# A two-layer streaming encoder on one core: first norm and first weight splits without GpSimd, and a scheduler with a transfer model and other TensorE prices

## The chip, the core and the metric

The program runs on one core of one Trainium2 chip. The metric is the device time of one execution in microseconds (us); for several runs it is the median. The engines are TensorE (PE; PEld is its weight load), VectorE (DVE), ScalarE (ACT), GpSimd (POOL) and SyncE (SP), which issues the DMAs. Each engine works through its own instructions in order and waits on semaphores for the others.

## The reference

A trunk of two layers over 512 frames, with 16 meta tokens ahead of them (528 rows of 1024 in all). Layer 0 projects the normed input once for two head groups, A (sparse attention with a top-k indexer) and B (gated linear attention in chunks of 64, "GLA"); layer 1 does so for C (retention) and D (stick-breaking attention). Cut to what matters here:

```python
def rms_norm(x, g):
    y = x * rsqrt(mean(x * x, -1) + 1e-6)
    return y * g
...
hn = rms_norm(h, norm_g[layer])
aq, ak, av, ag, iq, ik, iw, bq, bk, bv, bg, ba = split_cols(hn @ w_in, SPLIT_AB)
# indexer: score = sum_h relu(iq_h ik) * iw_h; top 128 keys of each frame, masked softmax over them
# B: chunked gated linear attention over bq, bk, bv with decays from ba
out = concat([oa * silu(ag), ob * silu(bg)]) @ w_out
h = h + out
```

Layer 1 has the same frame, and a last norm ends the program.

## The kernel before, in words

**Tiles and precision.** Everything stays on chip as 128x528 tiles. A projection of 128 output columns is 48 matmuls: eight blocks of 128 input features, three products each (upper part of the weights by upper part of x, upper by lower, lower by upper; the tiles are `wh`, `wl` for the weights, `hh`, `hl` for x, all in the rounded 32-bit format), each in two halves of 272 and 256 columns. An order row or a profile row `acc<-hh,wh` is such a product.

**Weights.** `load` (L541) brings half a projection's weights (128x512) into a `raw` tile. `split_next` (L562) makes `wh` from it, on GpSimd for the first `PW` tiles and on ACT after that, and `wl` = raw - wh, on GpSimd for the first `PL` tiles and on DVE after that. `PW, PL` stand in L482 as 2, 1. One projection, the "combined tile" (`COMB`, columns of indexer keys, indexer weights and GLA's gate), is put together from three transfers of 64, 8 and 16 columns into a tile that GpSimd has cleared.

**The start.** `consts` (L658) runs 46 warm-up transposes of the identity on PE (`WARM`, L483). `load_x` (L709) loads x in blocks of 128 rows, two 512-wide halves each (`pt`; the meta tokens in `gv`). For a block, `square` (L733) sums the squares of the first half on ACT and of the second half on DVE. `norm` (L744) takes Ln and Exp on ACT and scales the first half on DVE (L749) and the second on GpSimd (L750). `turn` (L752) transposes the blocks of one feature group on PE into a PSUM tile; ACT makes `hh` from it with the norm's gain, DVE makes `hl`. The products of the first indexer tile and of the combined tile are recorded between these steps.

**Order.** The code doesn't issue instructions directly. A recorder (`Recorder`) notes all of them with their dependences, and `issue` (L384) writes them out at the end in the order that a list scheduler finds; so all rows of recorded instructions carry the line of `issue`'s call, L393. `price` (L216) gives each an estimated cost and a matmul its class: contraction rows, plain or rounded operands, and slot length. `deadlines` (L260) walks the program once forward over PE (a matmul's due time is the sum of the slots ahead of it) and once backward (the latest start of every other instruction); these are the priorities. `order` (L285) then places instruction after instruction by the earliest start that its model of each engine gives, with priority among those that can start. `slot` (L376) adds `SWITCH` when PE goes from plain to rounded operands and `ROWS` when the contraction rows differ. Tiles rotate in pools (PSUM tags `x`, `y`, `acc`), and a buffer is given out in program order.

**Later stages.** After the first projections the indexer's scores are computed (about 36 to 80 us), then `topk` (L886) runs scans on DVE (`MAX`, `MATCH_REPLACE`) while PE goes on with values and GLA. `gla_steps` (L1318) is one GLA head: chunk products, a transpose of the key stack, then its meta step, which is a 16x16 product into a PSUM tile `m`, a masked copy of it by DVE (`attm`), a transpose of a 64x16 stack into the same tile, DVE's copy of that, and two small products. DVE then updates the head's state `ss` step by step. `out_ab` (L1410) ends layer 0, `stick` (L1590) is group D, `out_cd` (L1636) ends layer 1.

Of the kernel before, what the change touches and what calls it, by code (L numbers as in the profile page):

```python
# [13 lines left out]
ALU = mybir.AluOpType  # L14
# [152 lines left out]
class Recorder:  # L167
# [48 lines left out]
    def price(self, o):  # L216
        o.mm, o.port = None, False
        n = max([x.free() for x in o.ins + o.outs] or [1])
        sbuf = not any(x.tile.psum for x in o.ins)
        scalar = 65 if any(isinstance(x, View) and x.free() == 1 for x in o.ins) and n > 1 else 0  # L220
        if o.eng == "tensor":
            lhs, rhs = (o.args[1], o.args[2]) if len(o.args) > 2 else (o.kw["lhsT"], o.kw["rhs"])
            turn = o.name == "transpose"
            plain = rhs.dtype == F32
            k, m, n = lhs.shape[0], lhs.free(), rhs.free()
            two = plain and not turn
            o.mm = (k, plain, max(n * 0.455 * (2 if two else 1) + 4, 107 * m / P + 4) + (107 if two and n <= P else 0))
            o.cost = max(273, 170 + 0.4375 * n) if not two else 180 + 1.62 * n
        elif o.eng == "scalar":
            o.cost = (205 if sbuf else 165) + 0.83 * n + (80 if isinstance(o.kw.get("bias"), View) or isinstance(o.kw.get("scale"), View) else 0)  # L230
            if "accum_out" in o.kw:
                o.cost += 200
        elif o.eng == "vector":
            o.port = sbuf and o.name not in ("max", "match_replace")
            if o.name == "tensor_tensor_scan":
                o.cost = 144 + 2.1 * n
            elif o.name in ("tensor_scalar", "tensor_copy") and sbuf:
                o.cost = 160 + 0.52 * n + scalar
            elif o.name == "memset":
                o.cost = 100 + 0.3 * n  # L240
            else:
                o.cost = 148 + 1.05 * n + scalar
            if o.name == "tensor_tensor_reduce" or "accum_out" in o.kw:
                o.cost += 80
            if o.name == "match_replace":
                o.cost += 70
        elif o.eng == "gpsimd":
            o.cost = {"memset": 92 + 0.84 * n, "tensor_tensor": 178 + 2.17 * n}.get(o.name, 194 + 1.5 * n)
        else:
            x = o.outs[0] if o.outs else o.ins[0]  # L250
            kb = n * x.shape[0] / 256
            o.cost = 2000 + kb * (9 if any(y.tile.whole for y in o.outs + o.ins) else 3.5)


    LAT = {"tensor": 55, "vector": 33, "scalar": 34, "gpsimd": 60, "sync": 27}
    OVER = {"vector": -84, "scalar": -103, "gpsimd": -60}
    SWITCH, ROWS = 86, 50
    MARGIN = 300

    def deadlines(self):  # L260


        ops, t, last = self.ops, 0.0, None
        due = {}
        for o in ops:
            if o.eng == "tensor":
                if last is not None:
                    t += self.slot(last, o)
                last = o
            due[o] = t  # L270
        late = {}
        turn = {}
        for o in reversed(ops):
            end = min([late[q] - self.LAT[q.eng] for q in o.succs] + [late[q] - self.LAT[q.eng] for x in o.tiles
                      for q in [turn.get((x.kind, x.at + x.kind.bufs))] if q and q.at > o.at], default=due[o] + 20000)
            start = end - o.cost
            if o.eng == "tensor":
                start = min(start, due[o])
            late[o] = start
            for x in o.tiles:  # L280
                turn[x.kind, x.at] = o
        for o in ops:
            o.pri = due[o] if o.eng == "tensor" else late[o]

    def order(self):  # L285
        ops = self.ops
# [6 lines left out]
        free = dict.fromkeys(self.LAT, 0.0)  # L293
        lists = {e: [] for e in self.LAT}
        last = None
        begun = {}
        result = []

# [15 lines left out]
        while left:  # L314
            best = None
            for e, xs in lists.items():
                pick = None
                base = free[e] + (last.mm[2] if e == "tensor" and last is not None else 0)
                for o in xs:
# [11 lines left out]
                        continue  # L331
                    now = free[e] + (self.slot(last, o) if e == "tensor" and last is not None else 0)
                    start = max(est, now)
                    key = (max(est + (self.MARGIN if e == "tensor" else 0) - base, 0.0), o.pri)
                    if pick is None or key < pick[0]:
                        pick = (key, start, o)
                if pick and (best is None or pick[1] < best[1]):
# [5 lines left out]
            cost = o.cost  # L343
            if e == "vector" and o.port and begun.get("pool", (0, 0))[0] < start < begun.get("pool", (0, 0))[1] - 100:
                cost += begun["pool"][1] - start - 70
            end = start + cost
            ends[o] = end
            o.begin, o.end = start, end
            if e == "tensor":
                free[e], last = start, o  # L350
            elif e == "sync":
                free[e] = start + 430
            else:
                free[e] = end + self.OVER[e]
                if e == "gpsimd":
# [20 lines left out]
    def slot(self, a, b):  # L376
        t = a.mm[2]
        if a.mm[1] and not b.mm[1]:
            t += self.SWITCH
        if a.mm[0] != b.mm[0]:  # L380
            t += self.ROWS
        return t
# [14 lines left out]
class Kernel:  # L397
# [81 lines left out]
    LASTK = 4  # L479


    XL, XC, XN, XW, PW, PL = 2, 9, (0, 1, 1, 2), (1, 4, 7, 10, 13), 2, 1  # L482
    WARM = 46  # L483

    LAG = {"a": 5, "d": 6, "t": 1, "v": 4, "n": 9, "s": 6, "k": 11}
# [223 lines left out]
    def load_x(self):  # L709
# [34 lines left out]
        def norm(b):  # L744
# [2 lines left out]
            r = ms[b][:n]  # L747
            self.rstd(r, r, DM)
            nc.vector.tensor_scalar(x0[:n], x0[:n], r, None, op0=ALU.mult)  # L749
            nc.gpsimd.tensor_scalar(x1[:n], x1[:n], r, 1.0, op0=ALU.mult, op1=ALU.mult)  # L750

        def turn(group, t0, k):  # L752
            tr = self.s()
# [1039 lines left out]
```

## Time and profile before

| what | value |
|---|---|
| time of the kernel before, median of 3 | 663.05 us (662.98 to 663.65) |
| the profiled execution's own time | 663.46 us |
| its span, first to last instruction | 661.7 us |
| mean granted TensorE clock | 0.984 |
| instructions | 12217 |

Busy time over the span:

| engine | us | share | instructions |
|---|---|---|---|
| PE | 636.6 | 96% | 4469 |
| DVE | 484.3 | 73% | 1176 |
| ACT | 405.1 | 61% | 910 |
| POOL | 76.4 | 12% | 124 |

In a row of the timeline stand the start and the busy time, the engine, the line, the operation, what it writes and reads with shapes, and in brackets how long the engine stood idle before it and which engine's tile released it. In a row of the windows stand the stretch, then for PE, PEld, DVE, ACT and POOL the busy time with the count of instructions, then the granted clock as a share of the full one, the mean busy share of the DMA engines and the GB/s they moved. Durations of PE are modelled from pipelined matmuls, so a "busy" PE may be stalled behind a slow clock; spans on POOL are rough.

### The profile page before, as it was taken

What the parts mean: (1) busy time and instruction counts of PE and PEld (TensorE: products, weight loads), DVE (VectorE), ACT (ScalarE), POOL (GpSimd) and SP (SyncE); (2) the same over time, 40 slices, a digit from 0 to 9 for tenths busy, and PEclk for the clock granted to TensorE, in tenths of its full rate; (3) what the DMA queues carried; (4) which work ended last, traced back from release to release, by engine and by line L of the source; (5) the groups of instructions that cost most, each with busy time, mean ns of one, the idle gap of its engine ahead of it and who ended that gap; (6) DMA issues with size and microseconds to landing.
All of it is one profiled execution on the core that took longest, in us unless ns stands there. A gap on an engine that the chain in (4) does not pass through costs nothing.

```text
span 661.7 us, 12217 instructions
## 1 busy us (share of the span) xinstructions
PE 636.6 (96%) x4469; PEld 581.4 (88%) x4469; DVE 484.3 (73%) x1176; ACT 405.1 (61%) x910; POOL 76.4 (12%) x124
## 2 busy tenths in 40 slices
PE   5999999899999999999999999999999999999996
PEld 5879989798899999999899999878988888988884
DVE  4777799899987869679632764699935699955643
ACT  3656563353444877699643675799744699944434
POOL 7101110111000000001121110001200001110030
PEclk8899999799999999999999999999999999999998
DMA  7437222132322323112143272203322203224403
GB/s 217 118 83 224 72 74 72 46 96 65 81 57 75 98 65 97 52 47 65 50 145 112 67 238 81 64 21 93 97 65 64 78 2 104 83 71 149 153 17 127
DMA packets 91104, 59.25 MB, mean 90 GB/s; under 512 B 7315, under 2 KB 81629, under 8 KB 91045
## 3 DMA queue, kind: packets, MB, share of 16 engines
q1 hardware_dynamic: 91044, 58.48, 30.8%
q8 instruction: 35, 0.57, 0.3%
q14 instruction: 25, 0.20, 0.1%
HBM read 53.18 MB, written 6.90 MB: 91 GB/s over the span
## 4 chain that ended last, share of the span: by engine, by line
PE 67%; DVE 18%; ACT 9%; issue 2%; DMA 2%; SPq 0%; DVEq 0%; ACTq 0%
PE acc L393 45%; PE x L393 15%; PE y L393 6%; ACT wt L393 6%; DVE wt L393 5%; DVE st L393 3%; DVE lt L393 3%; DVE wl L393 3%; DVE m L393 2%; DMA pt<-in_x_dram 2%; ACT pt L393 1%; DVE pt L393 1%; ACT ptm L393 1%; ACT st L393 0%; DVE vt L393 0%
## 5 line engine op out<-in xcount | busy, mean ns | idle before, releaser
L393 PE MATMUL acc<-hh,wh 128*128 128x272 f32 (+2 forms) x968 | 246.5, 315 | 3.0 <-ACT hh L393 1.5
L393 PE MATMUL acc<-hh,wl 128*128 128x272 f32 (+2 forms) x968 | 234.2, 302 | 1.9 <-DVE wl L393 1.9
L393 PE MATMUL acc<-hl,wh 128*128 128x272 f32 (+2 forms) x968 | 234.8, 304 | 0.7 <-DVE hl L393 0.5
L393 ACT ACTIVATE wh<-raw 128x512 fp32r<-128x512 f32 x152 | 94.7, 629 | 125.2 <-PE acc L393 110.6
L393 PEld LDWEIGHTS acc<-hh,wh 128*128 128x128 f32 x968 | 159.5, 190 | 10.2 <-issue 3.0
L393 PEld LDWEIGHTS acc<-hh,wl 128*128 128x128 f32 x968 | 158.2, 190 | 8.5 <-DVE wl L393 2.8
L393 PEld LDWEIGHTS acc<-hl,wh 128*128 128x128 f32 x968 | 158.2, 190 | 5.0 <-DVE hl L393 1.5
L393 DVE TENSOR_TENSOR wl<-raw,wh 128x512 fp32r<-128x512 f32 x153 | 109.1, 718 | 57.2 <-ACT wh L393 52.2
L393 ACT ACTIVATE wt<-x 128x272 f32<-128x272 f32 (+3 forms) x100 | 43.0, 453 | 28.4 <-PE x L393 17.8
L393 POOL TENSOR_TENSOR gt<-gt,wt 128x528 f32<-128x528 f32 (+1 forms) x16 | 21.2, 1326 | 322.5 <-ACT wt L393 303.4
L393 PE MATMUL x<-st,st 128*128 128x272 f32 (+6 forms) x240 | 51.5, 292 | 0.1
L393 PE MATMUL x<-ident,wt 128*128 128x128 f32 (+2 forms) x300 | 46.0, 275 | 2.1 <-DVE wt L393 1.2
L393 ACT ACTIVATE wt<-wt 128x528 f32<-128x528 f32 (+3 forms) x74 | 42.9, 603 | 4.7 <-DVE wt L393 4.0
L393 PEld LDWEIGHTS x<-st,st 128*128 128x128 f32 (+2 forms) x240 | 37.5, 185 | 8.8 <-ACT wt L393 3.1
L393 ACT ACTIVATE wt<-wt,tiny 128x272 f32<-128x272 f32 (+5 forms) x64 | 34.7, 561 | 10.3 <-DVE tiny L393 10.0
L393 PEld LDWEIGHTS x<-ident,wt 128*128 128x128 f32 (+2 forms) x300 | 33.7, 139 | 7.0 <-DVE pt L393 1.4
L393 PE MATMUL y<-pt,vt 128*128 128x256 f32 (+1 forms) x288 | 38.6, 277 | 0.0
L393 PEld LDWEIGHTS y<-pt,vt 128*128 128x128 f32 x288 | 36.4, 189 | 1.3 <-DVE pt L393 0.7
L393 ACT ACTIVATE st<-acc 64x528 fp32r<-64x528 f32 (+1 forms) x58 | 34.7, 599 | 1.1 <-DVE lt L393 0.5
L393 DVE TENSOR_TENSOR_SCAN wt<-wt,wt 128x64 f32<-128x64 f32 (+5 forms) x50 | 30.8, 654 | 1.5 <-ACT wt L393 1.3
L393 DVE TENSOR_TENSOR pt<-x,pt 128x384 fp32r<-128x384 f32 (+1 forms) x48 | 28.1, 594 | 2.7 <-ACT pt L393 2.1
L393 ACT ACTIVATE wt<-wt,one 128x528 f32<-128x528 f32 (+3 forms) x42 | 29.5, 705 | 0.2
(191 smaller groups left out, 893.9 us busy)
## 6 DMA issues: line engine op xcount, KB each, us to landing
raw<-in_w_in_ab_dram SPq DMA_DIRECT2D x64, 256.0 KB, 2.8
raw<-in_w_in_cd_dram SPq DMA_DIRECT2D x56, 256.0 KB, 2.9
raw<-in_w_out_ab_dram SPq DMA_DIRECT2D x16, 256.0 KB, 2.8
raw<-in_w_out_cd_dram SPq DMA_DIRECT2D x16, 256.0 KB, 2.6
rep<-rows SPq DMA_DIRECT2D x8, 328.0 KB, 6.8
lt<-rep SPq DMA_DIRECT2D x8, 264.0 KB, 3.0
pt<-in_x_dram SPq DMA_DIRECT2D x8, 256.0 KB, 5.2
wt<-in_x_dram SPq DMA_DIRECT2D x8, 256.0 KB, 3.3
```

The costliest lines, as they stand in the source:

```text
L393: getattr(getattr(self.core, o.eng), o.name)(*[bind(x) for x in o.args], **{k: bind(x) for k, x in o.kw.items()})
```

## The change

It has two parts. In the kernel's code the second half of each block of x is scaled on DVE instead of GpSimd, and `PW, PL` are 0, 0: the first two upper weight tiles are made by ACT and the first lower one by DVE.

In the scheduler, nothing of what is computed differs, but the numbers and rules that set the order do. A matmul's class is 32, 64 or 128 contraction rows, and not the exact number; a slot is 0.45 ns per column. `SWITCH` is 80 and counts only after a matmul (10 after a transpose), `ROWS` is 95. A matmul whose row class is that of the one before gets 2000 ns (`STAY`) off its due time. A transfer's cost is its size times 3.6; the transfers share a modelled wire, so that each ends after the one before it and at least 1900 ns after its issue; one from scratch to scratch is taken at 6900 ns. The latest start of a transfer is set 3000 ns earlier, and SP issues in program order. A GpSimd instruction that starts beside a DVE instruction on the port they share is modelled as longer, where before only the reverse was. The call in `issue` now stands in L406.

```diff
-            o.mm = (k, plain, max(n * 0.455 * (2 if two else 1) + 4, 107 * m / P + 4) + (107 if two and n <= P else 0))
+            o.mm = (32 if k <= 32 else 64 if k <= 64 else P, plain, max(n * 0.45 * (2 if two else 1) + 4, 107 * m / P + 4) + (107 if two and n <= P else 0))
...
-            o.cost = 2000 + kb * (9 if any(y.tile.whole for y in o.outs + o.ins) else 3.5)
+            o.cost = kb * 3.6
...
-    SWITCH, ROWS = 86, 50
+    SWITCH, ROWS = 80, 95
     MARGIN = 300
+    STAY = 2000
...
-            start = end - o.cost
+            start = end - o.cost - (3000 if o.eng == "sync" else 0)
...
-            o.pri = due[o] if o.eng == "tensor" else late[o]
+            o.pri = due[o] if o.eng == "tensor" else o.at if o.eng == "sync" else late[o]
...
-                    key = (max(est + (self.MARGIN if e == "tensor" else 0) - base, 0.0), o.pri)
+                    pri = o.pri
+                    if e == "tensor" and last is not None:
+                        pri -= self.STAY if o.mm[0] == last.mm[0] else 0
+                    key = (max(est + (self.MARGIN if e == "tensor" else 0) - base, 0.0), pri)
...
+            if e == "gpsimd" and begun.get("port", (0, 0))[0] < start < begun.get("port", (0, 0))[1] - 100:
+                cost += begun["port"][1] - start - 100
             end = start + cost
+            if e == "vector" and o.port:
+                begun["port"] = (start, end)
...
                 free[e] = start + 430
+                wire = end = max(wire, start + 1900) + o.cost
+                if o.outs and o.outs[0].tile.whole and o.ins and o.ins[0].tile.whole:
+                    end = start + 6900
+                ends[o] = o.end = end
...
         if a.mm[1] and not b.mm[1]:
-            t += self.SWITCH
+            t += self.SWITCH if a.name == "matmul" else 10
...
-    XL, XC, XN, XW, PW, PL = 2, 9, (0, 1, 1, 2), (1, 4, 7, 10, 13), 2, 1
+    XL, XC, XN, XW, PW, PL = 2, 9, (0, 1, 1, 2), (1, 4, 7, 10, 13), 0, 0
...
-            nc.gpsimd.tensor_scalar(x1[:n], x1[:n], r, 1.0, op0=ALU.mult, op1=ALU.mult)
+            nc.vector.tensor_scalar(x1[:n], x1[:n], r, None, op0=ALU.mult)
```

What this does to the order is shown at three places; the number behind a tile's name is only its count in the recording and differs between the kernels.

GpSimd at the start, from the clearing of the mask constants on, before:

```order
L393 MEMSET ones 128x128
L393 TENSOR_SCALAR wh_259<-raw_202 128x512
L393 TENSOR_SCALAR gv_196<-gv_196,tiny_249 16x512
L393 TENSOR_TENSOR wl_284<-raw_202,wh_259 128x512
L393 TENSOR_SCALAR pt_157<-pt_157,tiny_270 128x512
L393 TENSOR_SCALAR wh_297<-raw_224 128x512
L393 TENSOR_SCALAR pt_177<-pt_177,tiny_299 128x512
L393 TENSOR_SCALAR pt_247<-pt_247,tiny_329 128x512
```

ACT at the same place after, from the read of the gains on (`raw_220` and `raw_230` are the first indexer tile's weights, `tiny_289` the scale of block 1, `wt_305` the square of block 2):

```order
L406 COPY gains<-x_268 128x18
L406 ACTIVATE wh_285<-raw_220 128x512
L406 ACTIVATE tiny_289<-tiny_289,eps 128x1
L406 ACTIVATE tiny_289<-tiny_289 128x1
L406 ACTIVATE wh_298<-raw_230 128x512
L406 ACTIVATE wt_305,tiny_306<-pt_238 128x512
L406 ACTIVATE hh_316<-x_270,gains 128x272
```

GpSimd's scalings and weight splits are gone (its rows are 113 instead of 121); ACT makes the two upper tiles between the norm's steps, and DVE has the scalings and the first lower split.

TensorE at its first products, before; `acc_336` is the first indexer tile, `acc_338` the combined tile:

```order
L393 MATMUL acc_336<-hh_327,wh_259 128x272
L393 MATMUL acc_338<-hh_327,wh_318 128x272
L393 MATMUL acc_336<-hl_341,wh_259 128x272
L393 MATMUL acc_336<-hh_327,wl_284 128x272
L393 MATMUL acc_336<-hh_327,wh_259 128x272
L393 MATMUL x_353<-ident,gv_185 128x16
```

After, where the combined tile (`acc_474`) begins:

```order
L406 MATMUL acc_322<-hl_325,wh_298 128x256
L406 MATMUL acc_322<-hh_316,wl_318 128x256
L406 MATMUL x_471<-ident,pt_250 128x128
L406 MATMUL acc_474<-hh_316,wh_456 128x272
L406 MATMUL acc_474<-hl_325,wh_456 128x272
L406 MATMUL x_471<-ident,pt_258 128x128
```

The combined tile's first product is row 13 of PE's order before and row 81 after. The first product of all is row 12 in both, and the first 512-wide product, behind both tiles, is row 139 in both.

TensorE at the meta step of the first GLA head, before; `x_1677` is the tile `m`, `acc_1679` the projection that goes on beside it:

```order
L393 MATMUL x_1677<-st_847,st_851 16x16
L393 MATMUL acc_1679<-hh_327,wh_1486 128x272
L393 MATMUL acc_1679<-hh_327,wh_1486 128x256
L393 MATMUL acc_1679<-hl_341,wh_1486 128x272
L393 MATMUL acc_1679<-hl_341,wh_1486 128x256
L393 MATMUL acc_1679<-hh_327,wl_1532 128x272
L393 MATMUL x_1677<-ident,st_853 16x64
```

After (`x_1697` is `m`, `x_1710` the state's chunk products):

```order
L406 MATMUL x_1697<-st_847,st_851 16x16
L406 MATMUL acc_1671<-hh_316,wh_1487 128x272
L406 MATMUL acc_1671<-hh_316,wh_1487 128x256
L406 MATMUL acc_1671<-hl_325,wh_1487 128x272
L406 MATMUL acc_1671<-hl_325,wh_1487 128x256
L406 MATMUL acc_1671<-hh_316,wl_1533 128x272
L406 MATMUL acc_1671<-hh_316,wl_1533 128x256
L406 MATMUL x_1710<-gv_1616,wt_1662 128x128 x2
L406 MATMUL x_1697<-ident,st_853 16x64
```

The 16x16 product moves from row 692 to 704 and the transpose behind it from 698 to 712. Over the whole program PE has the same 4317 matmuls; the row class changes 84 times instead of 90, and plain operands are followed by rounded ones 171 times instead of 173. On SP the x tiles and meta tokens come first, and the 8- and 16-column transfers of the combined tile move from rows 18 to 27 to rows 27 to 32.

More of the change, by code (lines that the diff above doesn't have):

```diff
@@ L295, in order @@
         last = None
+        wire = 0.0
         begun = {}
```

## Prediction

> **What bounds the kernel now.** I read the page first (engines, chain), then the windows by stage, then the timeline of the first 20 us, then the waits inside the stages.
>
> ```profile
> PE 636.6 (96%) x4469; PEld 581.4 (88%) x4469; DVE 484.3 (73%) x1176; ACT 405.1 (61%) x910; POOL 76.4 (12%) x124
> PE 67%; DVE 18%; ACT 9%; issue 2%; DMA 2%; SPq 0%; DVEq 0%; ACTq 0%
> ```
>
> TensorE (PE) is the bound over the whole program, and the chain of waits passes over VectorE (DVE) for 18%. The windows show where each of the two decides; the columns are the busy time of PE, PEld, DVE, ACT and POOL, then the granted clock.
>
> ```profile
> 0.00:12.70 12.70, 8.14 (x53) 7.77 (x53) 5.25 (x13) 4.91 (x14) 10.30 (x27) 1.00 0.79 229
> 12.70:22.90 10.20, 6.75 (x27) 4.99 (x25) 8.13 (x17) 5.45 (x15) 3.02 (x8) 0.50 0.74 179
> 80.00:122.00 42.00, 38.95 (x316) 37.79 (x314) 41.41 (x127) 21.36 (x52) 3.00 (x8) 1.00 0.28 70
> 121.90:128.70 6.80, 6.80 (x30) 5.82 (x30) 5.03 (x14) 0.76 (x3) 1.40 (x2) 0.50 0.16 39
> 128.70:190.00 61.30, 58.91 (x461) 54.99 (x461) 58.68 (x161) 24.88 (x50) 6.25 (x10) 1.00 0.27 70
> ```
>
> So there are two places to look at. In the head, up to 22.9 us, PE has little to do and a clock of 0.50; whatever starts its products earlier is worth its full time. From 80 to 190 us, where the top-k search runs beside GLA, DVE is busy for 41.41 of 42.00 and 58.68 of 61.30 us: there PE's own waits are mostly DVE's queue, and the stage can shrink by no more than DVE's idle time, 0.59 + 1.77 + 2.62 = 5.0 us.
>
> **The head, before.** The rows of the timeline from the warm-up transposes to the first products:
>
> ```profile
> 1.59 7.31 PE L393 MATMUL y<-ident 128*128 128x128 f32 x46 [1.59 <-POOL ident masks.py:199]
> ...
> 9.09 0.17 ACT L393 COPY gains<-x 128x18 f32<-128x18 f32 x1
> ...
> 10.21 0.61 ACT L393 ACTIVATE wt<-pt 128x512 f32<-128x512 f32 x1
> 10.34 1.99 DVE L393 TENSOR_SCALAR pt<-pt,tiny 128x512 f32<-128x512 f32 x1
> ...
> 10.73 0.19 ACT L393 ACTIVATION_READ_ACCUMULATOR wt<-pt 128x1 f32 x1
> ...
> 12.38 0.65 PE L393 MATMUL x<-ident,pt 128*128 128x128 f32 x3 [2.40 <-DVE pt L393]
> ...
> 12.91 0.29 ACT L393 ACTIVATE tiny<-tiny,eps 128x1 f32<-128x1 f32 x1 [2.00 <-DVE tiny L393]
> 13.24 0.20 ACT L393 ACTIVATE tiny<-tiny 128x1 f32<-128x1 f32 x1
> ...
> 13.48 1.43 DVE L393 TENSOR_SCALAR pt<-pt,tiny 128x512 f32<-128x512 f32 x1
> ...
> 16.23 0.63 ACT L393 ACTIVATE wh<-raw 128x512 fp32r<-128x512 f32 x1 [2.79 <-DMA raw<-in_w_in_ab_dram]
> 16.77 1.23 ACT L393 ACTIVATE hh<-x,gains 128x272 fp32r<-128x272 f32 x3
> 16.89 0.69 DVE L393 TENSOR_TENSOR wl<-raw,wh 128x512 fp32r<-128x512 f32 x1 [1.32 <-ACT wh L393]
> ...
> 17.38 0.79 PE L393 MATMUL acc<-hh,wh 128*128 128x272 f32 x2 [1.52 <-ACT hh L393]
> ...
> 17.50 1.31 DVE L393 SCALAR_TENSOR_TENSOR hl<-x,gains,hh 128x272 fp32r<-128x272 f32 x3
> ...
> 18.47 0.96 SPq L393 DMA_DIRECT2D wt<-in_c_bucket_dram x2
> ...
> 18.73 0.68 DVE L393 SCALAR_TENSOR_TENSOR wt<-pt 128x512 f32<-128x512 f32 x1
> ...
> 19.97 0.49 ACT L393 ACTIVATE hh<-x,gains 128x272 fp32r<-128x272 f32 x1 [0.38 <-PE x L393]
> ...
> 23.70 0.48 DVE L393 TENSOR_SCALAR pt<-pt,tiny 128x512 f32<-128x512 f32 x1
> ```
>
> The same scaling of a 128x512 tile takes DVE 1.99 and 1.43 us beside GpSimd's work and 0.48 us at 23.70. ACT then stands for 2.79 us at the combined tile's weights, with the first hh behind it. Two things that the change takes away from this place: GpSimd's five scalings and three weight splits, and the combined tile from its place ahead of the first hh.
>
> **The head, after, step by step.** The warm-up is unchanged, so the gains copy still ends at 9.09 + 0.17 = 9.26; the x tiles had been squared by then. ACT's order after it is: weight split 0.63, Ln and Exp of block 1 (12.91 to 13.44: 0.53), weight split 0.63, one square with its read-out (10.21 to 10.92: 0.71), first hh 0.49. That ends at 12.25. DVE beside it: split of the first weights 0.69 from 9.89, block 1 scaled in 0.48, so 11.06; three transposes 0.65: 11.7, in time for the hh at 11.76. The first product follows an hh by 0.12 (17.38 against 16.77 + 0.49): **12.4 instead of 17.4, 5.0 us earlier.**
>
> What then paces it to the end of the two first tiles, which is row 139 of PE's order in both kernels? Slots of PE by these rows:
>
> ```profile
> 33.83 0.28 PE L393 MATMUL acc<-hh,wl 128*128 128x256 f32 x1
> ...
> 36.04 0.40 PE L393 MATMUL acc<-hh,wh 128*128 128x512 f32 x1
> ```
> ```profile
> 471.18 0.60 PE L393 MATMUL x<-ident,wt 128*128 128x128 f32 x4
> ```
>
> From 33.83 to 36.04 stand 19 products: 0.12 each at the full clock; a transpose is (0.60 - 0.28) / 3 = 0.11. Row 139 is the one at 36.04. In the changed order, rows 12 to 80 hold 39 products and 30 transposes (8.0 us at the full clock, 16.0 at half), and the combined tile begins only at row 81, with 58 products or 7.0 us left. DVE up to the 13th hl that row 78 needs: from 11.06, two scalings 0.96, a split 0.69, 13 hl of 0.44 to 0.50, two squares of 0.75, four scalings 1.92, two small adds 0.3: 22.1 to 22.9. So:
> - Clock half until 19.5: PE has done 3.55 of its 8.0 us by then, the rest ends at 24.0, and row 139 stands at 31.0: a gain of 5.0. This is my value. The clock row above says 0.50 from 12.7 to 22.9, with the first product at 17.4, so it came back 5.5 us after the products began; from 12.4 that is 17.9 at the earliest, and 19.5 leaves room for the gaps between products.
> - Half until 22.9 as before: 5.2 us done, 25.7, row 139 at 32.7: 3.3.
> - Hardly any half clock: DVE paces, 22.9 and 7.0: 29.9, a gain of 6.1.
>
> The Trainium skill ("TensorE: Matmul & The Clock Gate", Part 1) says that the full clock returns after one busy window of about 3.4 us; by that the head would come out as in the last case, but the row shows 5.5 us, and I go by the row.
>
> The eight narrow transfers of the combined tile (8 and 16 columns) move on SP's queue from rows 18 to 27 back to rows 27 to 32, behind two whole weight tiles and the mask constants. SP's 32nd and 33rd transfers are the two bucket loads at 18.47, so the last piece is issued at about 19, and
>
> ```profile
> raw<-in_w_in_ab_dram SPq DMA_DIRECT2D x2, 32.0 KB, 2.5
> raw<-in_w_in_ab_dram SPq DMA_DIRECT2D x2, 16.0 KB, 2.7
> ```
>
> such pieces land 2.5 to 2.7 us after their issue: 21.7, ahead of the 24.0 at which row 81 wants them. Cost nothing, cover 2.3 us. What GpSimd gives up (four scalings and a 16-row one, three splits of the first weights) lies in the sums of ACT and DVE above; later GpSimd has only what it had.
>
> **The stage from 80 to 190 us.** The waits around the first GLA head's meta step, and one row of its third head:
>
> ```profile
> 119.38 0.29 PE L393 MATMUL acc<-hh,wl 128*128 128x272 f32 x1
> ```
> ```profile
> 121.50 0.14 DVE L393 COPY_PREDICATED attm<-tri,x 16x16 f32<-16x16 int32 x1
> ...
> 125.36 0.28 DVE L393 COPY st<-x 64x128 f32<-64x128 f32 x1 [0.77 <-PE x L393]
> ...
> 128.25 0.34 DVE L393 SCALAR_TENSOR_TENSOR st<-st,lt,x 64x128 f32<-64x128 f32 x1 [0.97 <-PE x L393]
> ```
> ```profile
> 121.71 0.22 PE L393 MATMUL x<-ident,st 64*16 64x64 f32 x1 [2.04 <-DVE attm L393]
> ...
> 188.12 0.69 DVE L393 TENSOR_TENSOR wl<-raw,wh 128x512 fp32r<-128x512 f32 x1
> ```
>
> PE stands for 2.04 us at a 64-row transpose because the small DVE copy ahead of it waits behind top-k scans; then the clock is 0.50 for 6.8 us. In the changed order this transpose is PE's row 712 instead of 698, so 14 products or 1.7 us more lie in front of it, while the copy's time is set by the scans ahead of it on DVE. PE's wait shrinks to 1 us or less and the clock may stay up, which is 1 + 3.4 us of PE's time. But DVE is full here. What the stage really gives is DVE's idle time that went with PE's lateness: 0.77 + 0.97 = 1.74 us. Against it, a weight split (0.69, the row at 188.12) now stands ahead of the third head's last state update. Sum 1.05; bounds 0 (the freed time is taken by other waits) and 5.0 (all of DVE's idle time).
>
> **Later.** Twice PE stands before transposes of pm:
>
> ```profile
> 473.69 0.28 PE L393 MATMUL x<-ident,pm 128*32 128x128 f32 x1 [0.48 <-DVE pm L393]
> ```
> ```profile
> 577.19 0.28 PE L393 MATMUL x<-ident,pm 128*32 128x128 f32 x1 [0.47 <-DVE pm L393]
> ```
>
> In the changed order these stand nine rows later and DVE's copy a split earlier, so both waits go: 0.95. Against it, at the end of layer 0 (312 to 316 us) two splits of the mix stand behind softmax steps on DVE, and products without cover are behind them: I put 0.45, between 0 and 1.4 (two of the 0.69 operations). Net 0.5. The order changes row groups 84 times instead of 90 and goes from plain to rounded operands 171 times instead of 173. That price no row shows alone; the six lie mostly in the stage where DVE is full, so I take 0 for it, at most 0.6 (0.1 each).
>
> **Sum.** 5.0 + 1.05 + 0.5 = 6.55 us. The profiled execution took 663.46 us, of which the span is 661.7 and 1.8 lies around it; it is 0.4 above the median of the three timed runs, 663.05. So 656.9 for it, and 656.5 on the scale of the median. A measurement of this kernel can tell about 0.2%, 1.3 us.
>
> **Rivals.**
> - *The clock stays down* (17%). Head 3.3, and the stage at 80 us gives 0.3: 4.1 with the later part, 659.0. For it: the row of 0.50 up to 22.9; rows 12 to 80 are thin, with DVE's hl between the products. The Trainium skill says in the same page, Part 4, that transposes don't count as PE activity for the clock; 30 of those 69 rows are transposes.
> - *PE gets all its time back* (13%): head 6.1, the stage near its 5.0 bound (4.2), 0.5 later: 10.8, 652.2. For it: without the 2.04 us wait nothing calls for the 0.50 after it. Against: DVE has 98.6% of the 42 us ahead of it.
> - *The gain is given back* (8%): the first products come early, but top-k and its releases are paced by something that doesn't move with them, or new waits of PE in the reordered rows eat it: 662 to 663, within 0.2%. The DVE window of 80 us and on speaks against, since top-k starts from the indexer's last score, which is PE's work of 36 to 80 us, and PE is busy there throughout.
> - *The combined tile's narrow pieces come late* (6%): rows 81 on wait for the last piece. From 24.0 each us is one us of the program; the gain of 6.55 is gone at 30.6, and at 33 us the time is 665.5. It would need a landing 14 us after issue instead of 2.7. GpSimd clears the two tiles ahead of these transfers, and each piece waits for the one before; that is what speaks for it.
>
> **How the numbers follow.** The forecast, with 56%, is 656.5; its own bounds are 654 to 659 (head 3.9 to 6.1, stage 0 to 2). The range reaches to the case in which PE gets nearly all back and to the middle of the low-clock case's far side: 652 to 660.5. Faster by over 0.2%: the first three cases, 86%. Within 0.2%: 8%. Slower: 6%.
>
> **What would show it.** Right: no scaling on GpSimd; DVE's 128x512 scalings near 0.5 us; first product near 12.4; the first 512-wide product, now at 36.04, near 31; the granted clock back by about 19.5; the wait before the 64-row transpose near 1 us; DVE still full from 75 to 185 us. Wrong, if the first product comes at 15 or later, if PE waits at the combined tile's first row for a transfer, if the clock is 0.50 up to 23 or again after the top-k waits, or if new waits over 0.5 us stand in PE's list after 190 us.

## The result, and the profile after

The changed kernel takes **652.74 us** (median of 4, 652.52 to 654.6) against 663.35 for the kernel before: ratio 0.9841, 95% interval 0.9822 to 0.9859. It is 10.6 us faster; I had forecast 6.55. The profiled execution took 654.6 us, with a span of 652.7. It is one of two kinds of execution that this kernel shows, 2 us apart; the clock makes the difference, as told below.

The page of after, engines and the chain's share by engine:

```profile
PE 633.3 (97%) x4469; PEld 582.8 (89%) x4469; DVE 483.5 (74%) x1182; ACT 406.3 (62%) x912; POOL 68.9 (11%) x116
PE 78%; DVE 12%; ACT 8%; issue 2%; POOL 0%; DVEq 0%; ACTq 0%; POOLq 0%
```

PE's busy time fell by only 3.3 us while the span fell by 9.0, so PE stands idle for 5.7 us less. The chain runs over PE for 78% instead of 67%, and over DVE for 12% instead of 18%; but this shift is one execution's. The second trace of the same kernel, told of below, has the shares of before back:

```profile
PE 71%; DVE 18%; ACT 8%; issue 3%; POOL 0%; DVEq 0%; ACTq 0%; POOLq 0%
```

The head after, from its timeline:

```profile
1.58 7.83 PE L406 MATMUL y<-ident 128*128 128x128 f32 x46 [1.58 <-POOL ident masks.py:199]
...
9.35 0.23 PE L406 MATMUL x<-ident,mid 18*128 18x18 f32 x1
...
9.61 0.17 ACT L406 COPY gains<-x 128x18 f32<-128x18 f32 x1 [2.08 <-PE x L406]
9.69 0.63 ACT L406 ACTIVATE wh<-raw 128x512 fp32r<-128x512 f32 x1
...
10.35 0.69 DVE L406 TENSOR_TENSOR wl<-raw,wh 128x512 fp32r<-128x512 f32 x1 [1.63 <-ACT wh L406]
...
10.96 1.27 DVE L406 TENSOR_SCALAR pt<-pt,tiny 128x512 f32<-128x512 f32 x3
...
11.50 0.55 PE L406 MATMUL x<-ident,pt 128*128 128x128 f32 x3 [0.95 <-DVE pt L406]
...
12.40 0.39 PE L406 MATMUL acc<-hh,wh 128*128 128x272 f32 x1 [0.36 <-ACT hh L406]
```
```profile
25.34 0.37 PE L406 MATMUL acc<-hh,wh 128*128 128x272 f32 x1
...
32.45 0.39 PE L406 MATMUL acc<-hh,wh 128*128 128x512 f32 x1
```

The first product stands at 12.40, where I had put it, by the chain that I had written down. The hit is in part luck: the gains copy ended at 9.78 and not at 9.26, and the steps behind it, which overlap, took 0.4 us less than my sum of them. DVE's three scalings take 1.27 together. The combined tile's first product is at 25.34 (forecast 24.0), the first 512-wide product at 32.45 (31.0). New is ACT's wait of 2.08 us for the gains: it waits for the end of the warm-up transposes, which the work before had hidden.

The windows after; the last figures of a row are the granted clock, the DMA share and GB/s:

```profile
12.10:13.70 1.60, 0.79 (x4) 0.59 (x4) 1.60 (x5) 1.00 (x3) 0.00 (x0) 1.00 1.09 295
13.70:20.60 6.90, 6.90 (x31) 5.81 (x30) 4.92 (x14) 3.16 (x10) 0.00 (x0) 0.51 0.75 172
20.60:22.90 2.30, 2.30 (x18) 2.07 (x18) 1.68 (x4) 1.76 (x4) 0.00 (x0) 1.00 0.00 0
...
119.60:126.40 6.80, 6.80 (x30) 5.82 (x30) 5.92 (x18) 1.40 (x4) 0.03 (x1) 0.50 0.22 56
```

The half clock of the head now ends at 20.6, and that of the stage is still there, 6.8 us long. The wait in front of it, from the timeline:

```profile
119.02 0.14 DVE L406 COPY_PREDICATED attm<-tri,x 16x16 f32<-16x16 int32 x1
...
119.22 0.22 PE L406 MATMUL x<-ident,st 64*16 64x64 f32 x1 [1.68 <-DVE attm L406]
```

The wait shrank from 2.04 to 1.68, not to 1 or less. Two rows from the second half of the program, where PE stood 0.48 and 0.47 us before the change:

```profile
468.37 0.27 PE L406 MATMUL x<-ident,pm 128*32 128x128 f32 x1
```
```profile
569.67 0.27 PE L406 MATMUL x<-ident,pm 128*32 128x128 f32 x1
```

Both waits are gone, as forecast.

**Where the time came from.** I added up PE's instructions in each trace at the spacing that they have when nothing delays them (0.45 ns a column and 3 ns for a product, 109 ns for a 128-wide transpose), and read at which time each trace reaches the same sum. The lead over before's trace:

| trace | head, up to 66 us | 66 to 234 us | 234 us to the end | total |
|---|---|---|---|---|
| forecast | 5.0 | 1.05 | 0.5 | 6.55 |
| after, first trace | 3.55 | -0.13 | 5.62 | 9.04 |

Stretches are given in times of before. Head and stage came out smaller than I said: the head inside its bounds (3.3 to 6.1), the stage just below its lower one (0). The rest, for which I had 0.5 us, gave 5.6.

### The profile page after: what moved, and what is told of

Read it like the earlier page. It is cut to its first block, busy times and chain, and to the rows that moved or that the text cites. A ratio compares the mean times of both kernels' runs of the same rounds, so it can differ in the third digit from the quotient of the medians.

```text
span 652.7 us, 12208 instructions
## 1 busy us (share of the span) xinstructions
PE 633.3 (97%) x4469; PEld 582.8 (89%) x4469; DVE 483.5 (74%) x1182; ACT 406.3 (62%) x912; POOL 68.9 (11%) x116
## 4 chain that ended last, share of the span: by engine, by line
PE 78%; DVE 12%; ACT 8%; issue 2%; POOL 0%; DVEq 0%; ACTq 0%; POOLq 0%
PE acc L406 53%; PE x L406 17%; PE y L406 8%; ACT wt L406 4%; DVE st L406 2%; DVE wt L406 2%; DVE wl L406 2%; DVE lt L406 1%; ACT st L406 1%; DVE pt L406 1%; DVE m L406 1%; ACT wh L406 1%; DVE kl L406 1%; ACT ptm L406 1%; ACT pt L406 1%
## 5 line engine op out<-in xcount | busy, mean ns | idle before, releaser
L406 PE MATMUL acc<-hh,wh 128*128 128x272 f32 (+2 forms) x968 | 244.8, 314 | 1.4 <-DVE lt L406 0.4
L406 PE MATMUL acc<-hl,wh 128*128 128x272 f32 (+2 forms) x968 | 236.4, 305 | 0.9 <-DVE hl L406 0.9
L406 PE MATMUL acc<-hh,wl 128*128 128x272 f32 (+2 forms) x968 | 234.6, 303 | 2.1 <-DVE wl L406 2.1
L406 ACT ACTIVATE wh<-raw 128x512 fp32r<-128x512 f32 x154 | 96.1, 631 | 121.5 <-PE acc L406 107.7
L406 PEld LDWEIGHTS acc<-hh,wh 128*128 128x128 f32 x968 | 159.5, 190 | 8.5 <-issue 0.9
L406 PEld LDWEIGHTS acc<-hh,wl 128*128 128x128 f32 x968 | 158.5, 190 | 8.7 <-DVE wl L406 2.9
L406 PEld LDWEIGHTS acc<-hl,wh 128*128 128x128 f32 x968 | 158.6, 190 | 5.4 <-DVE hl L406 1.7
L406 DVE TENSOR_TENSOR wl<-raw,wh 128x512 fp32r<-128x512 f32 x154 | 109.7, 717 | 63.0 <-ACT wh L406 60.7
L406 ACT ACTIVATE wt<-x 128x272 f32<-128x272 f32 (+3 forms) x100 | 43.1, 454 | 24.4 <-PE x L406 15.7
L406 POOL TENSOR_TENSOR gt<-gt,wt 128x528 f32<-128x528 f32 (+1 forms) x16 | 21.7, 1355 | 331.0 <-ACT wt L406 309.7
L406 PE MATMUL x<-st,st 128*128 128x272 f32 (+6 forms) x240 | 50.9, 290 | 0.0
L406 PE MATMUL x<-ident,wt 128*128 128x128 f32 (+2 forms) x300 | 46.0, 274 | 2.0 <-DVE wt L406 1.2
L406 ACT ACTIVATE wt<-wt 128x528 f32<-128x528 f32 (+3 forms) x74 | 43.2, 606 | 3.9 <-DVE wt L406 3.3
L406 PEld LDWEIGHTS x<-st,st 128*128 128x128 f32 (+2 forms) x240 | 37.3, 185 | 7.1 <-ACT wt L406 2.5
L406 ACT ACTIVATE wt<-wt,tiny 128x272 f32<-128x272 f32 (+5 forms) x64 | 34.6, 562 | 9.3 <-DVE tiny L406 8.8
L406 PEld LDWEIGHTS x<-ident,wt 128*128 128x128 f32 (+2 forms) x300 | 34.5, 139 | 6.4 <-DVE pt L406 1.4
L406 PE MATMUL y<-pt,vt 128*128 128x256 f32 (+1 forms) x288 | 39.4, 279 | 0.2 <-DVE pt L406 0.2
L406 PEld LDWEIGHTS y<-pt,vt 128*128 128x128 f32 x288 | 36.6, 190 | 0.9 <-DVE pt L406 0.5
L406 ACT ACTIVATE st<-acc 64x528 fp32r<-64x528 f32 (+1 forms) x58 | 34.7, 599 | 1.0 <-DVE lt L406 0.4
L406 DVE TENSOR_TENSOR_SCAN wt<-wt,wt 128x64 f32<-128x64 f32 (+5 forms) x50 | 30.9, 657 | 2.1 <-ACT wt L406 1.7
L406 ACT ACTIVATE wt<-wt,one 128x528 f32<-128x528 f32 (+3 forms) x42 | 29.5, 704 | 0.2
L406 DVE TENSOR_TENSOR pt<-x,pt 128x384 fp32r<-128x384 f32 (+1 forms) x48 | 28.1, 596 | 1.8 <-ACT pt L406 0.9
```

The lines of the kernel that those rows point to most:

```text
L406: getattr(getattr(self.core, o.eng), o.name)(*[bind(x) for x in o.args], **{k: bind(x) for k, x in o.kw.items()})
```

## The experiments

My theory before them: GpSimd's scalings and splits and the combined tile's early place hold up the head; what is gained behind 234 us comes from PE's new prices. The rivals: the head comes from the transfers' order; the late gain is chance of one execution.

**The changed kernel again**, without an edit.

> The changed kernel itself, unaltered, for a second trace and more executions. In the first trace the half clock stood in stretches of 6.83 us (13.76 to 20.59 and 119.58 to 126.40), that execution took 654.6 us at a mean clock of 0.986, and three others took 652.5 to 652.8 at 0.992. Theory of the free-running window: the clock is decided on a grid of 3.41 us whose phase differs between executions, so executions come in two groups about 2 us apart, and in a trace of the faster group one of the two stretches (or half of each) is missing. Rival, everything before 36 us is fixed by the program: every trace has both stretches, and 654.6 was a disturbance elsewhere.

Five executions: 651.97, 652.24 and 652.41 us at a mean clock of 0.991 to 0.992, and 654.34 and 654.4 at 0.986 to 0.987 (ratio of all 0.9838, 0.9816 to 0.9861). The second trace is one of the first group. Its windows:

```profile
12.10:13.70 1.60, 1.18 (x4) 0.91 (x4) 1.60 (x4) 0.23 (x1) 0.00 (x0) 0.52 1.15 329
13.70:20.60 6.90, 6.90 (x37) 6.13 (x36) 4.52 (x14) 3.98 (x12) 0.00 (x0) 0.62 0.70 151
...
116.20:119.60 3.40, 1.71 (x14) 1.40 (x12) 3.40 (x10) 0.26 (x1) 2.29 (x2) 1.00 0.32 76
119.60:126.40 6.80, 6.64 (x53) 5.90 (x51) 6.44 (x18) 2.39 (x6) 0.00 (x0) 1.00 0.18 40
```

and the wait:

```profile
118.42 0.22 PE L406 MATMUL x<-ident,st 64*16 64x64 f32 x1 [1.69 <-DVE attm L406]
```

The same wait, 1.69 us, and no half clock behind it. The clock's own records in the trace say why. In before's trace the clock changes at 12.69, 22.93, 121.91 and 128.74 us, in after's at 13.76, 20.59, 119.58 and 126.40, in this one at 12.15 and 18.98. Every distance is a multiple of 3.413 us (10.24 = 3, 6.83 = 2, 98.99 = 29), and the grid's place against the program's start differs from trace to trace. In after's first trace the wait lies from 117.54 to 119.22, whole in the step from 116.16 to 119.58. In the second one it lies from 116.73 to 118.42 across the step's border at 117.96, with 1.23 us before and 0.46 behind. The Trainium skill ("TensorE: Matmul & The Clock Gate", Part 1) states such a free-running window of 3413 ns; the traces agree. It also says that the clock drops after at least one idle window: here a wait of 1.68 us inside one was enough. All 14 traces of this document bear that out. Up to 640 us, 22 steps at the full clock hold 1.58 us or more in which no PE row is busy, and a half clock follows every one of them. From 1.45 to 1.54 us both occur, and of the steps with less a single one was followed by a half clock (1.01 us, in the transfers' kernel below).

The lead of this trace is 4.37 in the head, 1.28 in the stage and 5.57 behind it, 11.22 in all. The late gain agrees to 0.05 us: it is no chance of one execution. The head differs by 0.82 us, and that is the grid too. The warm-up transposes start 213 ns apart until the full clock's first record, at 6.94 us in after's trace and at 5.32 in this one, and 109 ns apart from there; so ACT's gains copy and the first product come earlier here (11.62 instead of 12.40). In the stage this trace's lead over before rose by 3.3 us around the wait (4.99 at 116 us, 8.28 at 130), and 2.6 of that were lost by 234 us (5.64): its waits for DVE's states are longer, 2.7 us against 1.0 in before. From the lists of PE's waits, after and again (sum, times, longest):

```profile
PE y L406 <- DVE st L406: 1.7, 4, 0.9
```
```profile
PE y L406 <- DVE st L406: 2.7, 6, 0.9
```

That is the full DVE, 6.44 of 6.80 us in the window above.

**The code's part alone**: the kernel before with

```diff
-            nc.gpsimd.tensor_scalar(x1[:n], x1[:n], r, 1.0, op0=ALU.mult, op1=ALU.mult)
+            nc.vector.tensor_scalar(x1[:n], x1[:n], r, None, op0=ALU.mult)
...
-    XL, XC, XN, XW, PW, PL = 2, 9, (0, 1, 1, 2), (1, 4, 7, 10, 13), 2, 1
+    XL, XC, XN, XW, PW, PL = 2, 9, (0, 1, 1, 2), (1, 4, 7, 10, 13), 0, 0
```

> The kernel before with the second half of x scaled on DVE and PW, PL = 0, 0; its scheduler is unaltered (combined tile begins at PE row 31). My account of the head: the first product comes near 12.5 and the gain is made in the head alone, 3.0 to 4.5 us: 658.5 to 660.5. Rival, the head's gain needs the new order of transfers and the combined tile behind the first one: the first product near 15 or later, 661 to 663. After 320 us nothing should differ from before in either.

661.82 us, ratio 0.9974 (0.9961 to 0.9987): the rival's time, though the first product comes earlier than it said. From its timeline:

```profile
14.04 0.59 PE L393 MATMUL acc<-hh,wh 128*128 128x272 f32 x1 [0.15 <-ACT hh L393]
...
34.31 0.47 PE L393 MATMUL acc<-hh,wh 128*128 128x512 f32 x1 [0.39 <-DVE st L393]
```

Taking GpSimd out brings the first product from 17.38 to 14.04, and 1.7 us at the end of the head; behind 234 us nothing (-0.10).

**The transfers' part alone**: the kernel before with

```diff
-            o.cost = 2000 + kb * (9 if any(y.tile.whole for y in o.outs + o.ins) else 3.5)
+            o.cost = kb * 3.6
...
-            start = end - o.cost
+            start = end - o.cost - (3000 if o.eng == "sync" else 0)
...
-            o.pri = due[o] if o.eng == "tensor" else late[o]
+            o.pri = due[o] if o.eng == "tensor" else o.at if o.eng == "sync" else late[o]
...
+                wire = end = max(wire, start + 1900) + o.cost
```

and the modelled wire's other lines.

> The kernel before with the transfers' part alone: cost, wire, 3000 ns earlier, program order on SP; the code and PE's prices unaltered (combined tile begins at PE row 68). If the head's gain of the new scheduler (2.4 us) comes from the transfers and the place of the combined tile, it is here: 660.5 to 661.7. If it comes from GpSimd's modelled port or PE's prices, 662.5 to 663.7. Behind 100 us nothing in both.

660.48 us, ratio 0.9949 (0.9932 to 0.9965): the first case, at its edge.

```profile
11.63 0.55 PE L398 MATMUL acc<-hh,wh 128*128 128x272 f32 x1 [1.05 <-ACT hh L398]
...
33.15 0.40 PE L398 MATMUL acc<-hh,wh 128*128 128x512 f32 x1
```

With GpSimd's scalings still in place the first product is at 11.63, and the head gains 2.9 us. So the order of the transfers (x first, then the first weights, the combined tile late) brings the first product forward by itself; in this kernel GpSimd's scalings don't prevent that. My account of the head named the right rows but priced this part at nothing. In this trace the clock is also at half from 90.16 to 93.58 us, which takes 1.5 us of the lead back; behind 100 us 0.5 comes.

**The new scheduler alone**: the changed kernel with the two lines of the code's part put back.

> The changed kernel with the scaling back on GpSimd and PW, PL = 2, 1: the new scheduler alone. Theory that GpSimd's work at the start is what the head waited for: the first product stays near 16 to 17 and the head gives 0 to 1 us; the part of the gain behind 320 us (5 us in the trace) stays, since PE's order there is the same as in the changed kernel: 657 to 658.5. Rival, that the scheduler's part is worth only what I forecast behind 80 us (1.5 us): 661 to 662.

655.66 us, ratio 0.9871 (0.9851 to 0.9891), faster than both cases. The head gains 2.43 (first product at 15.24, first 512-wide one at 33.61), the part behind 234 us the whole 5.70. The scheduler is 8 of the 10.6 us. With GpSimd at work the whole new scheduler has its first product 3.6 us later than the transfers' part alone (11.63), and taking GpSimd out brings it from 15.24 to 12.40. So in the changed kernel the early product does need GpSimd out of the way. Which of the scheduler's other edits takes back what the transfers gave, no run shows.

**Without the new PE prices**: the changed kernel with

```diff
-            o.mm = (32 if k <= 32 else 64 if k <= 64 else P, plain, max(n * 0.45 * (2 if two else 1) + 4, 107 * m / P + 4) + (107 if two and n <= P else 0))
+            o.mm = (k, plain, max(n * 0.455 * (2 if two else 1) + 4, 107 * m / P + 4) + (107 if two and n <= P else 0))
...
-    SWITCH, ROWS = 80, 95
+    SWITCH, ROWS = 86, 50
...
-            t += self.SWITCH if a.name == "matmul" else 10
+            t += self.SWITCH
```

and no `STAY`.

> The changed kernel with the old prices of PE (exact contraction rows, 0.455, SWITCH 86, ROWS 50, no STAY); transfers and the kernel's code as changed. If STAY and ROWS make the gain behind 320 us, it is lost here: 656.5 to 658. If that gain comes from the other parts (transfers, priorities), it stays: 652 to 654. The head should be as in the changed kernel in both, row 139 near 32.5.

657.8 us, ratio 0.9907 (0.989 to 0.9925). The head keeps 3.51; behind 234 us 1.35 of 5.6 are left. PE's prices make 4.3 us there. The two waits before `pm` (0.95 us) are gone in this kernel too, so they may be most of what is left.

**Which price?** Five kernels, each the changed one with some of them put back. The columns are the ratio with its interval and the lead in the three stretches.

| kernel | put back | ratio | head | to 234 | to the end |
|---|---|---|---|---|---|
| stay0 | `STAY = 0` | 0.9872 (0.9844 to 0.9899) | 4.21 | -0.17 | 4.55 |
| stay_cls | `SWITCH, ROWS = 86, 50`, SWITCH behind transposes too | 0.9912 (0.9893 to 0.9931) | 3.18 | -0.80 | 2.37 |
| sw_old | SWITCH behind transposes too | 0.9899 (0.9883 to 0.9915) | 3.84 | -0.57 | 3.46 |
| sw_only | all PE prices of before but the 10 behind transposes | 0.9915 (0.9887 to 0.9943) | 3.93 | 0.42 | 1.87 |
| rows50 | `ROWS = 50` | 0.989 (0.9864 to 0.9917) | 2.97 | -2.14 | 5.60 |

> The changed kernel with STAY = 0; SWITCH 80, ROWS 95, the row classes and the transfers as changed. Without all of the new PE prices the gain behind 250 us fell from 5.6 to 1.4 us. If keeping products over the same rows together (STAY) makes it, this kernel falls back as far: 656.5 to 658. If the dearer change of rows (ROWS 95) does it in the slots' sum, it keeps 4 us or more of it: 652 to 654.

> The changed kernel with SWITCH 86 and ROWS 50 back, the switch counted after transposes too; STAY = 2000, the row classes and the transfers as changed. The other side of the test before: if STAY makes the gain behind 250 us, 652 to 654; if ROWS and SWITCH make it, 656.5 to 658.

> The changed kernel, with SWITCH counted after a transpose as before (80 instead of 10); all else as changed. From 250 us to the end the changed kernel gains 5.6 us, and 1.4 us without all new PE prices; STAY = 0 left 4.5 us of it, STAY without SWITCH and ROWS 2.4 us. If the price behind a transpose is what counts, about 3 us go here: 655 to 656.5. If ROWS 95 is, this kernel stays at 652 to 654.

> The changed kernel with all PE prices of before but one: SWITCH isn't counted after a transpose (10). Transfers and the kernel's code as changed. If this price alone makes most of the gain behind 250 us: 653.5 to 655.5. If it needs the other prices with it: 656.5 to 658, as without any of them.

> The changed kernel with ROWS 50 as before; STAY, SWITCH, row classes, 0.45 and the transfers as changed. Behind 224 us the changed kernel gains 5.6 us; without STAY 4.55, with SWITCH behind transposes 3.5, without either of ROWS and SWITCH 2.4. If ROWS carries a part of its own, 1 us or more goes here too (653.5 to 655.5). If STAY already does what ROWS would, since both speak against a change of rows, the time stays at 652 to 653.3.

654.85, 658.22, 656.89, 657.66 and 656.59 us. Only the fourth lies in a range that I had given; my readings were too simple. Behind 234 us the largest single price is the `SWITCH` behind a transpose, 10 ns now: putting back the 80 costs 2.2 of 5.6 us. `STAY` is worth 1.1. Alone the first gives only 0.5 over the 1.35 (sw_only), `STAY` with the classes 1.0 (stay_cls); together they give 4.3 (rows50 has both, and the whole 5.60). `ROWS` gives nothing there, but without it the stage with the full DVE loses 2.14 us of the lead instead of 0.13; from its list of PE's waits:

```profile
PE x L406 <- DVE attm L406: 2.9, 1, 2.9
```

The wait at the meta step grew to 2.9 us, though PE's two rows there (780 and 792 of the trace) are those of after. From the timelines, after and rows50:

```profile
117.33 0.68 DVE L406 TENSOR_TENSOR wl<-raw,wh 128x512 fp32r<-128x512 f32 x1
117.36 1.80 POOL L406 TENSOR_TENSOR gt<-gt,wt 128x528 f32<-128x528 f32 x1 [16.99 <-ACT wt L406]
```
```profile
117.96 1.29 POOL L406 TENSOR_TENSOR gt<-gt,wt 128x528 f32<-128x528 f32 x1 [16.93 <-ACT wt L406]
118.00 1.80 DVE L406 TENSOR_TENSOR wl<-raw,wh 128x512 fp32r<-128x512 f32 x1
```

In after DVE's weight split begins 0.03 us ahead of GpSimd's product, and GpSimd's is the longer one; in rows50 it begins 0.04 us behind it and takes 1.80 us instead of 0.68, with the masked copy behind it. So 1.1 us of rows50's loss in the stage come from this meeting of DVE and GpSimd, and are no price of a change of rows.

What the truer prices do behind 234 us can be counted in PE's spacings. The short delays there aren't in the list of waits, since a PE row's busy time is modelled and covers them; they show as the distance from one start to the next. From the timeline of after:

```profile
558.81 0.29 PE L406 MATMUL acc<-hh,wh 128*128 128x272 f32 x1
558.94 0.49 PE L406 MATMUL x<-ident,wt 128*128 128x128 f32 x3
559.19 0.37 PE L406 MATMUL acc<-hh,wh 128*128 128x256 f32 x1
559.39 0.41 PE L406 MATMUL acc<-hl,wh 128*128 128x272 f32 x2
```

The 256-wide product at 559.19 has 0.20 us to its successor instead of 0.12, and no row shows an idle time. But this one is no loss: the three transposes ahead of it took 0.25 us instead of 0.33, so the product began 0.08 early. A delay that nothing makes up for is the product at 530.18, with 0.22 us to its successor instead of 0.12:

```profile
530.06 0.28 PE L406 MATMUL y<-pt,vt 128*128 128x256 f32 x1
530.18 0.38 PE L406 MATMUL x<-st,st 128*128 128x256 f32 x1
530.40 0.28 PE L406 MATMUL x<-kl,st 128*128 128x256 f32 x1
```

Counted over the stretch; the lower row holds both kinds:

| from 234 us on | before | no_pe | sw_old | stay0 | after |
|---|---|---|---|---|---|
| instructions with a semaphore wait, over 0.04 us late | 93, 14.5 us | 91, 13.4 | 91, 12.5 | 82, 12.2 | 81, 11.8 |
| products without a wait, over 0.06 us late | 135, 12.3 us | 135, 12.3 | 133, 12.1 | 118, 10.8 | 119, 10.8 |

Twelve waits and sixteen short delays fewer are 2.65 + 1.55 of the 5.6 us; the rest is in transposes (0.6 from a transpose to a product, 0.45 between transposes) and in changes of rows (0.35). The short delays repeat: after's two traces both show 119. But a recount of the lower row by the same spacings (138 in before, 124 in after) finds the kind of 559.19 in 82 and 85 of them: there a spacing was short by as much one or two places ahead, mostly between a transpose and a product, and no time is lost. 56 (5.7 us) and 39 (4.0 us) are real delays of about 0.1 us, so the difference stands (1.7 us here), but not the 12.3. Of the real ones 31 and 21 follow directly on an instruction that itself had a semaphore to wait for. What makes them stays open; no run here takes them apart.

**A tile of its own for the meta step's transpose**: the changed kernel with

```diff
-        self.transpose(m[:NMETA, 32:96], kh[0:64, :NMETA])
+        mk = self.tr()
+        self.transpose(mk[:NMETA, 32:96], kh[0:64, :NMETA])
...
-        nc.vector.tensor_copy(ktm, m[:NMETA, 32:96])
+        nc.vector.tensor_copy(ktm, mk[:NMETA, 32:96])
```

> The changed kernel, with the transpose of the GLA head's meta step in a PSUM tile of its own, so that it no longer waits for DVE's masked copy of the 16x16 product (PE's wait of 1.68 us at 117.5 us). Theory: that wait inside one window of the clock's grid is what halves the clock from 120 to 126 us in some executions; without it no execution has that stretch, every one shows a mean clock of 0.991 or more, and the time is 650.5 to 652.0 with no second group at 654.4. Rival: PE comes to stand as long at the next product that needs DVE's copies, the clock falls as before, 652 to 654.5.

651.56 us (650.85 to 651.76), ratio 0.9812 (0.9798 to 0.9827).

```profile
119.19 0.43 PE L406 MATMUL x<-vm,mid 16*64 16x128 f32 x2 [1.47 <-DVE attm L406]
```

Partly the rival: the wait moved to the next product that needs DVE, at 1.47 us. In this trace (mean clock 0.994) the clock did not fall in the stage. Two other executions have 0.992 and 0.993, one has 0.987 and took 651.72. No execution was near 654.4, but four are few: that the wait's new place spares the clock is not shown.

**Ten warm-up transposes fewer**, on top of that: `WARM = 36` in place of 46.

> The changed kernel with the meta step's transpose in a tile of its own and WARM = 36 instead of 46. In both traces of the changed kernel ACT's read of the gains waits for the end of the warm-up transposes (1.04 and 2.08 us), and the first weight split, the scaling of block 1 and the first product stand behind it. If that chain sets the head, ten transposes less bring the first product 1 to 1.6 us earlier and the time to 650 to 651 (651.56 with 46). If the clock falls earlier for it, or the x tiles' and weights' landing sets the head, 651.3 to 653.

650.55 us (648.89 to 652.06), ratio 0.9804 (0.9778 to 0.983): the lowest median, but its interval holds that of the kernel with 46. Its timeline shows the rival:

```profile
7.92 0.17 ACT L406 COPY gains<-x 128x18 f32<-128x18 f32 x1
...
9.08 0.63 ACT L406 ACTIVATE wh<-raw 128x512 fp32r<-128x512 f32 x1 [0.99 <-DMA raw<-in_w_in_ab_dram]
...
11.79 0.60 PE L406 MATMUL acc<-hh,wh 128*128 128x272 f32 x1 [0.36 <-ACT hh L406]
```

The gains come 1.7 us earlier, and then ACT waits for the first weights' landing, at 9.08. The times follow the clock: 648.89 at a mean of 0.999, 652.06 at 0.987.

## Why the prediction was right, and which terms were off

- **The bound.** PE over the whole, DVE in the stage with top-k: right. The second trace shows it best, where 2.6 us that PE had gained are lost again, 1.7 of them in longer waits for DVE's states.
- **First product at 12.4.** Measured 12.40 and 11.62. The chain was right, its start at 9.26 was not: the warm-up's pace hangs on the clock's grid, and the gains copy ended at 9.78 and 9.00. That only GpSimd stands in the way was not right either: the transfers' order alone gives 11.63, the code alone 14.04. In the new scheduler GpSimd does stand in it (15.24 with its work put back).
- **Head, 5.0 us.** 3.55 and 4.37, inside the bounds of 3.3 and 6.1. The clock was back at 20.59 and 18.98, for which I had 19.5; the products up to row 80 ended at 25.34 instead of 24.0. The last 58 products took 7.11 us (forecast 7.0).
- **Cost nothing, the narrow transfers.** Right: the combined tile's splits on ACT follow an hh at once, with no wait for a transfer, and the rival of the late pieces did not occur. But the same reordering of transfers was an edit with a gain that I never priced.
- **Stage, 1.05 us.** -0.13 and 1.28, by where the grid lies; the first is just outside the bounds of 0 and 5.0. The wait didn't shrink to 1 us. PE came to it 2.13 us earlier than before (117.54 against 119.67), for the products now ahead of it cost part of the head's gain, but DVE's copy came 2.49 us earlier as well, and only 0.36 was left.
- **Later, 0.5 us.** This is the term that failed: 5.6 us. The 0.95 for the two waits before pm was right: both are gone, without PE's prices too. The step that failed is "I take 0 for it, at most 0.6 (0.1 each)": I priced six changes of rows and two of kind one by one, and read the list of waits behind 190 us as all there was to gain. But PE's spacings behind 234 us hold some 25 us of delay in before's trace, where PE's idle time sums up to 5.1, and the new scheduler put another operation at 548 of the 2848 places in PE's trace there. That took 5.6 us off, 4.3 of them by PE's prices.
- **Rivals.** The time is that of "PE gets all its time back", 652.2, but not its mechanism: the stage stayed far from its 5.0. It lies outside the forecast's own bounds (654 to 659) and in the range only because that reached down to this rival: there the prediction had luck, since a gain that it put at nothing made up for a head and a stage that gave less. The clock did stay down in the stage in some executions; between the two traces that and the head's 0.82 make 2.2 us, where I gave the case 2.5. One of my signs of being wrong, a clock of 0.50 again after the top-k waits, so came true in the first trace. That transposes don't count for the clock, which I quoted for this case, does not show here: up to 8.6 us PE had run nothing but the warm-up transposes in before's trace, and from 5.86 us on they stood 109 ns apart instead of 213. Nothing was given back in whole.

## What to carry to other kernels

A PE that is shown 96% busy may still hold several per cent of delay; read it from start to start before saying that nothing is left, and over two or three spacings, since a late start can only make up for an early one. In a list scheduler the price of a common pair (transpose, then product) can be worth more than a penalty on a rare one: here it was 2.2 us, if only together with `STAY`. Why it works so, whether by keeping the model's time right for all that follows, is not shown. And test an edit that "costs nothing" by itself: the transfers' order alone gave 2.9 us of the head, the code's part alone 1.7.

## What the runs showed of the hardware

- The half clock comes and goes on a grid of 3.413 us that isn't tied to the program's start. A wait of about 1.7 us halved the clock for 6.83 us when it lay in one step of the grid and did not when it was split 1.23 to 0.46. Executions of one kernel so differ by 2 us (652.4 against 654.4); in the two traces 0.8 of that come from the warm-up's end and 1.4 from the stage.
- A half clock lasted one, two or three steps: 3.41 us in the kernel with 36 warm-ups, behind its wait of 1.47; 6.83 us in most; 10.24 us at the head of before. A wait of 1.47 us, whole in one step too, was followed by none in the kernel with the transpose's own tile.
- Behind a transpose a rounded product costs no extra: in before's trace from 234 us on, 39 such pairs without a wait (128x128 transposes) stood 28 ns apart, 81 ns closer than the 109 ns that a transpose has from another, and the next spacing was 80 to 94 ns too long.
- Transposes alone brought the full clock: in before's trace the warm-up's stood 213 ns apart up to 5.86 us and 109 ns from there, with nothing else on PE.
- A weight split on DVE beside a GpSimd product took 0.68 us in after, where it began 0.03 us ahead of it, and 1.80 us in rows50, where it began 0.04 us behind it.
